# Two groups of weight transfers get later due times in a kernel whose order a list schedule makes

## The chip, the cores and the metric

The kernel runs on one core of a Trainium2 chip. Its time is device microseconds of one execution. A measurement is the median of several executions; three of the kernel before gave 621.62 us (621.21 to 625.1).

## The reference

One decoder layer in float32 on 512 tokens of width 1024: a mixing part (retention heads beside sparse attention) with an output projection, and a gated feed-forward part with a short causal convolution. What the change touches lies in the second half:

```python
mix = jnp.concatenate([y_ret, y_nsa], axis=-1) @ w_out[l]
x = x + rms_norm(mix, norm_mix_post[l])
h = rms_norm(x, norm_ffn_pre[l])
x = x + rms_norm(conv_ffn(h, ffn_w_up[l], ffn_conv[l], ffn_w_down[l]), norm_ffn_post[l])

def conv_ffn(x, w_up, conv_w, w_down):        # w_up: 1024 x 5632, w_down: 2816 x 1024
    u = x @ w_up
    u = depthwise_causal_conv(u, conv_w)       # width 3
    gate, val = jnp.split(u, 2, axis=-1)
    return (jax.nn.gelu(gate) * val) @ w_down
```

## The kernel before

**Arithmetic.** Each float32 matrix is split into a rounded high part (a copy on ScalarE, ACT) and the rest as a low part (a subtraction on VectorE, DVE), and each product is three matmuls: high by high, high by low, low by high.

**Order.** The body doesn't issue instructions. It records operations in a `_Plan`, and `schedule` (L262) orders them: each engine (TensorE as PE, ACT, DVE, GpSimd as POOL, SyncE as SP) has a clock, each operation a cost from `cost`, and of the operations that could start within 20 ns (`SLACK`, L32) of an engine's earliest one the plan takes that with the lowest rank, which within this part of the kernel is the one written first. `emit` then issues each engine's instructions in that order, and the hardware runs each engine's queue strictly in it. So an assumed time shows in the program only as an order: an instruction that the plan believed ready can stand in a queue ahead of one that is ready in fact.

**Due times of transfers.** A transfer's issue costs 475 ns on SP and 1000 ns on POOL. Then it is due at (L368, L369)

```python
dma = max(dma, op.end) + nbytes / (175.0 if "accum_op" in k else 350.0)
op.end = dma + (4000 if e == POOL else 2000) + op.late
```

in nanoseconds, with bytes per nanosecond as the divisors. `op.late` is what `plan.late` was when the operation was recorded (L191); nothing else reads it. `plan.late` is 0 but for the loads of the up stage, where it is 800 (`LATE`, L1386).

**Stage h2.** After the attention part, `wo1(t)` (L1179) makes the second half of the output projection for the 128 tokens of t, 24 matmuls. It squares and sums the result on ACT (`junk<-wo`), and goes on to the norm (`r`, with a power on POOL), the residual sum (`mix<-mix,r,xres`), the square of that (`xres<-mix`), and the next norm (`xres<-mix,r,wpre`). `h2(t)` (L1216) transposes that on PE (`tp<-cn,xres`) into `h2h` and `h2l`. In PE's order of rank wo1 of the later t and the first up products stand behind, and can fill in.

**First up weights.** `ws` (L1342, L1343) loads four blocks of the up weights, 512 KB each, on SP's queue into tile `raw` (two buffers) and splits each: three in one piece (`wh<-raw` on ACT, `wl<-raw` on DVE), the second in two pieces (`w<-raw`, `w<-raw,w`). They are recorded behind wo1 and h2. `up` (L1240) multiplies with them, for column blocks 0 and 1 of gate and value.

**Up stage.** The 20 remaining pairs of column blocks, i = 2 to 21, are made by seven products each (a Strassen form), in the order 1, 2, 6, 5, 7, 3, 4 (`strassen`, L1310), 12 matmuls each. In the trace they are `X<-h2h,b`, `G<-h2h,b`, `X<-T,b`, `G<-T,b`, `X<-T,b`, `G<-h2h,b`, `X<-h2h,b`. The seventh, named "4", uses the tile `w["4"]` (tag av, four buffers, which the tiles a of a11 and a12 share). `loads(i+1)` (L1283) is recorded ahead of the products of i; it issues three transfers on SP and four on POOL, 256 KB each. Two of POOL's add into s1 and s3. The third, here called the casting transfer, copies the second half of the value weights into `w["4"][:, 1]` and rounds it on the way. Behind it ACT writes its negative into `w["4"][:, 0]`, and the fourth, an accumulating transfer, adds the unrounded weights to that, which leaves the low part. `prep` (L1299) makes the parts of the other six products on ACT and DVE (`b<-b`).

**Down stage.** `t_sums`, `product` and what follows do the same for the down weights. The same schedule orders it.

Of the kernel before, what the change touches and what calls it, by code (L numbers as in the profile page):

```python
# [402 lines left out]
def _body(ctx, tc, io, out, soff, coff):  # L403
# [5 lines left out]
    plan = _Plan(nc)  # L409
# [6 lines left out]
    def nm(s):  # L416
        cnt[0] += 1
        return f"{s}_{cnt[0]}"

    def s4(shape, dt=F32, n="s"):  # L420
        return plan.tile(gp, shape, dt, nm(n), "s4", 12)
# [4 lines left out]
    def vv(shape, dt=F32, n="v"):  # L426
        return plan.tile(gp, shape, dt, nm(n), "vv", 2)
# [23 lines left out]
    def acc(n="acc"):  # L451
        return plan.tile(pp, [P, 512], F32, nm(n), "acc", 4)
# [7 lines left out]
    def copy(o, i, scale=None, engs="A"):  # L460
        k = {} if scale is None else {"scale": scale}
        alts = {}
        if "A" in engs:
            alts[ACT] = ("activation", (o, i, AF.Copy), k)
        for c, e in (("D", DVE), ("P", POOL)):
            if c in engs and scale is None:
                alts[e] = ("tensor_copy", (o, i), {})
            elif c in engs and e == POOL:
                alts[e] = ("tensor_tensor", (o, i, scale.to_broadcast(list(o.shape))), {"op": ALU.mult})
            elif c in engs:  # L470
                alts[e] = ("tensor_scalar", (o, i, scale, None), {"op0": ALU.mult})
        plan.add(alts)

    def f(ap):
        return ap.bitcast(F32)
# [34 lines left out]
    def nextw(src, a, b, eng=dve_pool, **k):  # L510
        return splitw(loadw(src, a, b, **k), eng=eng)
# [136 lines left out]
    def transpose4(bank, src):  # L648
        m = bank("tp").rearrange("p (a b) -> p a b", a=4)
        for q in range(4):  # L650
            transpose(m[:, q, :], src(q))
        return m
# [497 lines left out]
    def rawtile(shape=(P, 2, 512)):  # L1150
        return plan.tile(st, list(shape), F32, nm("raw"), "raw", 2)

    def rows(src, a, b):

        return [[x[:, k, :] for k in range(a)] for x in nextw(src, a, b, eng=dve)]

    def rows2(src, a, b, alloc):

        raw, n = rawtile((P, a, b)), a // 2
        sync.dma_start(raw, src)  # L1160
        parts = [], []
        for q in range(2):
            hi, lo = (alloc([P, n, b], F32R, "w") for _ in range(2))
            copy(hi, raw[:, q * n:q * n + n])
            dve.tensor_tensor(lo, raw[:, q * n:q * n + n], f(hi), op=ALU.subtract)
            for k in range(n):
                parts[0].append(hi[:, k, :])
                parts[1].append(lo[:, k, :])
        return parts
# [9 lines left out]
    def wo1(t):  # L1179
        ts = slice(t * P, (t + 1) * P)  # L1180
        a = acc("wo1")
        for j in range(4):
            for b in range(2):
                mm3(a, yh[j][:, b, ts], yl[j][:, b, ts], w1p[j][0][b], w1p[j][1][b],
                    j == 0 and b == 0, j == 3 and b == 1)
        act.activation(junk, a, AF.Square, accum_out=sm2[:, t, 1:2])
        r = tiny([P, 6], "r1")
        dve.tensor_tensor(r[:, 0:1], sm2[:, t, 0:1], sm2[:, t, 1:2], op=ALU.add)
        dve.tensor_scalar(r[:, 0:1], r[:, 0:1], 1.0 / D, 1e-6, op0=ALU.mult, op1=ALU.add)
        rsqrt(r[:, 1:2], r[:, 0:1], 1)  # L1190
        xr = (vv if t < 2 else s4)([P, D], n="xres")
        sync.dma_start(xr, io["x"][ts, :])
        dve.tensor_tensor(mix[t][:, 512:1024], a, wpost[:, 512:1024], op=ALU.mult)
        for c in range(2):
            cs = slice(512 * c, 512 * c + 512)
            dve.scalar_tensor_tensor(mix[t][:, cs], mix[t][:, cs], r[:, 1:2], xr[:, cs], op0=ALU.mult, op1=ALU.add)
            act.activation(xr[:, cs], mix[t][:, cs], AF.Square, accum_out=r[:, 4 + c:5 + c])
        spills.append(sync.dma_start(io["x2"][ts, :], mix[t]))
        dve.tensor_tensor(r[:, 2:3], r[:, 4:5], r[:, 5:6], op=ALU.add)
        dve.tensor_scalar(r[:, 2:3], r[:, 2:3], 1.0 / D, 1e-6, op0=ALU.mult, op1=ALU.add)  # L1200
        rsqrt(r[:, 3:4], r[:, 2:3], 1)
        for c in range(2):
            cs = slice(512 * c, 512 * c + 512)
            dve.scalar_tensor_tensor(xr[:, cs], mix[t][:, cs], r[:, 3:4], wpre[:, cs], op0=ALU.mult, op1=ALU.mult)
        hns[t] = xr
# [10 lines left out]
    def h2(t):  # L1216
        ts = slice(t * P, (t + 1) * P)
        rs = slice(t % 2 * P, t % 2 * P + P)
        if t == 2:
            t13.extend(vv([P, 4, HT], n="T") for _ in range(2))  # L1220
        for q in range(2):
            m = transpose4(mps, lambda k: hns[t][:, (4 * q + k) * P:(4 * q + k + 1) * P])
            copy(h2h[q][:, :, ts], m)
            dve.tensor_tensor(h2l[q][:, :, ts], m, f(h2h[q][:, :, ts]), op=ALU.subtract)
            if t < 2:
                for a in range(2):
                    copy(hb[q][a][:, :, rs], m[:, 2 * a:2 * a + 2, :])
            elif q:
                dve.tensor_tensor(t13[1][:, :, rs], t13[1][:, :, rs], m, op=ALU.subtract)
            else:  # L1230
                for a in range(2):
                    k = slice(2 * a, 2 * a + 2)
                    dve.tensor_tensor(t13[0][:, k, rs], m[:, k, :], hb[0][a][:, :, rs], op=ALU.subtract)
                copy(t13[1][:, :, rs], m)
# [45 lines left out]
    def blk(pool, tag, bufs, dt=F32R):  # L1280
        return plan.tile(pool, [P, 2, 4, P], dt, nm("b"), tag, bufs)

    def loads(i):  # L1283
        g, v = io["wup"][i, 0], io["wup"][i, 1]
        a, s13 = blk(gp, "av", 4, F32), blk(st, "raw", 2, F32)
        w = {"4": blk(gp, "av", 4)}
        a11, a12, s1, s3 = a[:, 0], a[:, 1], s13[:, 0], s13[:, 1]
        sync.dma_start(a11, g[:, 0:4])
        sync.dma_start(s1, v[:, 0:4])
        sync.dma_start(a12, g[:, 4:8])  # L1290
        pool.dma_start(s1, v[:, 4:8], accum_op=ALU.add)
        copy(s3, a11, scale=-1.0)
        pool.dma_start(s3, v[:, 0:4], accum_op=ALU.add)
        pool.dma_start(w["4"][:, 1], v[:, 4:8])
        copy(w["4"][:, 0], f(w["4"][:, 1]), scale=-1.0)
        pool.dma_start(w["4"][:, 0], v[:, 4:8], accum_op=ALU.add)
        return a11, a12, s1, s3, w
# [39 lines left out]
    for t in range(NT):  # L1337
        wo1(t)
        h2(t)
    ws = [rows(io["wup"][0, 0], KT, P), rows2(io["wup"][0, 1], KT, P, pt),  # L1340
          rows(io["wup"][1, 0], KT, P), rows(io["wup"][1, 1], KT, P)]
    ab = [acc("up") for _ in range(4)]  # L1342
    for c0 in (0, 256):  # L1343
        for i in range(4):
# [41 lines left out]
    LATE = 800  # L1386
    plan.late = LATE
    nxt = loads(PL)
    plan.late = 0
    for i in range(PL, NF):  # L1390
        now = prep(*nxt)
        if i == PL:
            glu(1, ab[2], ab[3])
        if i + 1 < NF:
            plan.late = LATE
            nxt = loads(i + 1)
            plan.late = 0
        else:
            uv = u_parts(0), v_parts(0)
        glu(i, *strassen(i, now))  # L1400
# [129 lines left out]
    late = [pair[:, 0], pair[:, 1], s4([P, 2, 512], n="late")]  # L1530
# [46 lines left out]
```

## Time and profile before

| | us |
|---|---|
| median of three runs | 621.62 |
| the profiled execution | 626.48 |
| its span | 624.7 |
| outside the span | 1.8 |
| PE busy | 606.3 |
| DVE busy | 536.8 |
| ACT busy | 426.6 |
| POOL busy | 173.5 |

The profiled execution is 4.86 us above the median. On the page matmuls are pipelined, so the busy time of PE is no measure of its peak; the idle time of PE, by what ended it, is read from the waits. Nearly every instruction is issued from line 398 (`emit`), so groups are told apart by tiles, and where a tile name is shared (`b`), by form and place in time.

### The profile page before, as it was taken

Reading aid. Unit: us, or ns where it says so; the run is one execution under the profiler, and the core shown is the slowest. Engines: PE = TensorE matmul, PEld = TensorE weight load, DVE = VectorE, ACT = ScalarE, POOL = GpSimd, SP = SyncE. Lnnn points to the kernel's source line nnn. Section 1 sums busy time; section 2 is a strip of 40 time slices with the busy share of each in tenths; the row PEclk is TensorE's granted clock in tenths of the full one; section 3 lists DMA queues with packets and bytes.
Section 4 is the critical chain, followed back from the end, with each engine's and each line's share of the span. In section 5 each row is a group of like instructions: output and inputs, shape, how many; then the busy total and the mean of one; then the engine's idle time right before and its main releaser. Section 6 shows DMA issues by size and latency. Waiting matters only on the chain. (4 is left out here: it accounts for less than half of the span.)

```text
span 624.7 us, 10841 instructions
## 1 busy us (share of the span) xinstructions
PE 606.3 (97%) x3782; PEld 537.1 (86%) x3782; DVE 536.8 (86%) x1142; ACT 426.6 (68%) x872; POOL 173.5 (28%) x200
## 2 busy tenths in 40 slices
PE   8998999999999999999999999999999999999995
PEld 5787988888878888789999999999999987787884
DVE  5589877997888885589999989999999999889994
ACT  6735657778998645475867767675777667678761
POOL 0003532533215320032123232324241222231070
PEclk9999899999999999999999999999999999999999
DMA  8762366525126517447467877788868579997722
GB/s 277 298 239 88 135 169 147 124 40 129 35 68 134 137 35 269 164 147 179 93 143 176 180 190 168 182 176 194 204 148 198 121 187 216 238 214 247 268 91 102
DMA packets 42103, 102.31 MB, mean 164 GB/s; under 512 B 4672, under 2 KB 5056, under 8 KB 42048
## 3 DMA queue, kind: packets, MB, share of 16 engines
q0 software_dynamic: 18576, 41.16, 33.8%
q1 hardware_dynamic: 23184, 60.06, 27.9%
q8 instruction: 30, 0.49, 0.3%
q10 hardware_dynamic: 288, 0.39, 0.2%
q14 instruction: 25, 0.20, 0.1%
HBM read 97.40 MB, written 4.19 MB: 163 GB/s over the span
## 5 line engine op out<-in xcount | busy, mean ns | idle before, releaser
L398 DVE TENSOR_TENSOR b<-b,b 128x512 fp32r<-128x512 f32 (+1 forms) x160 | 103.8, 683 | 2.8 <-ACT b L398 1.7
L398 POOL DMA_DIRECT2D b<-wup x80 | 63.5, 930 | 153.3 <-ACT b L398 82.8
L398 ACT ACTIVATE b<-b 128x512 fp32r<-128x512 f32 (+1 forms) x160 | 92.2, 623 | 12.4 <-DMA b<-wup 5.3
L398 PE MATMUL acc<-wl,xh 128*128 128x512 f32 (+1 forms) x192 | 72.8, 384 | 0.6 <-DVE wl L398 0.6
L398 PE MATMUL acc<-wh,xh 128*128 128x512 f32 (+1 forms) x192 | 72.4, 385 | 0.3 <-ACT kc L398 0.3
L398 PE MATMUL acc<-wh,xl 128*128 128x512 f32 (+1 forms) x192 | 72.6, 383 | 0.0
L398 PE MATMUL G<-h2h,b 128*128 128x256 f32 x320 | 64.6, 284 | 0.9 <-ACT b L398 0.9
L398 PE MATMUL X<-T,b 128*128 128x256 f32 x480 | 64.9, 284 | 0.2
L398 PE MATMUL X<-h2h,b 128*128 128x256 f32 x320 | 61.4, 284 | 0.5 <-DVE X L398 0.5
L398 PEld LDWEIGHTS X<-T,b 128*128 128x128 f32 x480 | 60.5, 192 | 0.8 <-DVE b L398 0.6
L398 DVE TENSOR_TENSOR wl<-raw,wh 128x1024 fp32r<-128x1024 f32 (+1 forms) x40 | 48.8, 1221 | 9.9 <-ACT wh L398 9.7
L398 PEld LDWEIGHTS G<-h2h,b 128*128 128x128 f32 x320 | 52.9, 192 | 1.3 <-ACT b L398 1.3
L398 ACT ACTIVATE wh<-raw 128x1024 fp32r<-128x1024 f32 (+2 forms) x43 | 43.1, 1008 | 15.9 <-issue 6.4
L398 PEld LDWEIGHTS X<-h2h,b 128*128 128x128 f32 x320 | 51.4, 192 | 1.0 <-DVE X L398 0.9
L398 PE MATMUL G<-h2l,b 128*128 128x256 f32 x160 | 45.3, 283 | 0.0
L398 PE MATMUL X<-h2l,b 128*128 128x256 f32 x160 | 45.3, 283 | 0.0
L398 PEld LDWEIGHTS acc<-wh,xh 128*128 128x128 f32 x192 | 36.5, 191 | 6.5 <-ACT kc L398 0.7
L398 PEld LDWEIGHTS acc<-wl,xh 128*128 128x128 f32 x192 | 36.6, 191 | 6.4 <-DVE wl L398 1.4
L398 PEld LDWEIGHTS acc<-wh,xl 128*128 128x128 f32 x192 | 36.7, 191 | 5.2
L398 ACT ACTIVATE P<-P,nmx 128x256 f32<-128x256 f32 (+3 forms) x64 | 35.2, 551 | 6.6 <-DVE nmx L398 6.5
L398 PE MATMUL d<-wl,ah 128*128 128x512 f32 x88 | 34.4, 394 | 2.4 <-DVE wl L398 2.4
L398 POOL DMA_DIRECT2D T<-wdn x21 | 18.1, 878 | 57.0 <-ACT T L398 49.8
(298 smaller groups left out, 1646.9 us busy)
## 6 DMA issues: line engine op xcount, KB each, us to landing
b<-wup POOLq DMA_DIRECT2D x80, 256.0 KB, 5.2
b<-wup SPq DMA_DIRECT2D x60, 256.0 KB, 5.1
raw<-wdn SPq DMA_DIRECT2D x15, 512.0 KB, 5.8
T<-wdn POOLq DMA_DIRECT2D x21, 256.0 KB, 6.3
T<-wdn SPq DMA_DIRECT2D x10, 256.0 KB, 5.7
xnat<-x SPq DMA_DIRECT2D x4, 512.0 KB, 7.1
raw<-w_nq SPq DMA_DIRECT2D x4, 512.0 KB, 6.0
raw<-w1k SPq DMA_DIRECT2D x4, 512.0 KB, 5.2
```

The source lines that it names most:

```text
L398: i = getattr(getattr(self.nc, op.eng), method)(*a, **k)
```

## The change

The casting transfer of `loads` is recorded with a `late` of 4500 ns where it had 800, and the four loads of the first up weights with 2000 where they had 0. No operation is added or taken away, none changes its size, queue, buffers or recorded place. The plan's due times change, and with them the order that it makes from there on.

```diff
@@ loads(i)
         copy(s3, a11, scale=-1.0)
         pool.dma_start(s3, v[:, 0:4], accum_op=ALU.add)
+        late, plan.late = plan.late, max(plan.late, 4500)
         pool.dma_start(w["4"][:, 1], v[:, 4:8])
+        plan.late = late
         copy(w["4"][:, 0], f(w["4"][:, 1]), scale=-1.0)
         pool.dma_start(w["4"][:, 0], v[:, 4:8], accum_op=ALU.add)
@@ _body
     for t in range(NT):
         wo1(t)
         h2(t)
+    plan.late = 2000
     ws = [rows(io["wup"][0, 0], KT, P), rows2(io["wup"][0, 1], KT, P, pt),
           rows(io["wup"][1, 0], KT, P), rows(io["wup"][1, 1], KT, P)]
+    plan.late = 0
     ab = [acc("up") for _ in range(4)]
```

## Rows read from the trace of the kernel before

**Rows 1.** The page's first part: busy us of an engine, its share of the span, and its instructions.

```profile
PE 606.3 (97%) x3782; PEld 537.1 (86%) x3782; DVE 536.8 (86%) x1142; ACT 426.6 (68%) x872; POOL 173.5 (28%) x200
```

**Rows 2.** Busy time by stretches (us from the span's start): length, then busy us of PE, PEld, DVE, ACT, POOL with instructions, granted clock, DMA share, GB/s. The stretches are stage h2, the rest of it with the first up products, the up stage in part, and the down stage.

```profile
262.00:277.00 15.00, 13.50 (x68) 10.80 (x67) 11.86 (x24) 10.38 (x25) 3.77 (x6) 1.00 0.41 152
277.00:302.00 25.00, 24.82 (x207) 24.57 (x206) 23.08 (x42) 17.17 (x34) 7.77 (x10) 1.00 0.65 157
...
402.00:452.00 50.00, 49.48 (x409) 49.03 (x409) 47.67 (x82) 35.68 (x70) 15.89 (x20) 1.00 0.80 181
...
525.00:614.00 89.00, 86.63 (x379) 70.37 (x378) 81.35 (x131) 62.73 (x112) 25.41 (x17) 1.00 0.73 206
```

**Rows 3.** What PE waited for from 245 us to the end (the waits of 245 to 302, of 300 to 510, and of 502 to 625 us): us in total, times, longest.

```profile
PE tp L398 <- DVE xres L398: 1.5, 1, 1.5
...
PE G L398 <- ACT b L398: 0.9, 2, 0.6
PE X L398 <- DVE X L398: 0.5, 1, 0.5
...
PE d L398 <- DVE wl L398: 2.4, 3, 1.0
PE d L398 <- ACT wh L398: 0.8, 2, 0.7
```

**Rows 4.** The first and the second of the four loads of the first up weights: the issue in the timeline of SP (start, duration), and in the view of the DMA issues its KB and us from issue to landing. The third and the fourth took 3.2 and 3.1.

```profile
251.41 0.33 SPq L398 DMA_DIRECT2D raw<-wup  x1
raw<-wup SPq DMA_DIRECT2D x1, 512.0 KB, 3.3
253.22 0.33 SPq L398 DMA_DIRECT2D raw<-wup  x1
raw<-wup SPq DMA_DIRECT2D x1, 512.0 KB, 5.7
```

**Rows 5.** Timeline of ACT in stage h2: start, duration, what, and idle time before with what ended it.

```profile
254.83 1.06 ACT L398 ACTIVATE wh<-raw 128x1024 fp32r<-128x1024 f32 x1 [0.25 <-DMA raw<-wup]
258.98 0.63 ACT L398 ACTIVATE w<-raw 128x512 fp32r<-128x512 f32 x1 [3.09 <-DMA raw<-wup]
259.52 0.58 ACT L398 ACTIVATE junk<-wo 128x512 bf16<-128x512 f32 x1
```

**Rows 6.** Timeline of PE there: the first and the last of the 24 matmuls of `wo1(0)`, the last one ahead of the transposes, the first transposes, and the first up product.

```profile
252.01 0.39 PE L398 MATMUL wo<-wh,yh 128*128 128x512 f32 x1
...
257.22 0.39 PE L398 MATMUL wo<-w,yl 128*128 128x512 f32 x1
...
264.25 0.39 PE L398 MATMUL wo<-wh,yh 128*128 128x512 f32 x1
266.14 0.66 PE L398 MATMUL tp<-cn,xres 128*128 128x128 f32 x4 [1.50 <-DVE xres L398]
...
277.44 0.28 PE L398 MATMUL up<-h2h,wh 128*128 128x256 f32 x1
```

**Rows 7.** Timeline of DVE there: the chain from the sum of squares to the transposes' input, with the two subtractions of the second load.

```profile
259.64 0.69 DVE L398 TENSOR_TENSOR w<-raw,w 128x512 fp32r<-128x512 f32 x1 [2.50 <-ACT w L398]
260.25 0.15 DVE L398 TENSOR_TENSOR r<-sm 128x1 f32<-128x1 f32 x1
260.32 0.68 DVE L398 TENSOR_TENSOR mix<-wo,wpost 128x512 f32<-128x512 f32 x1
260.92 0.14 DVE L398 TENSOR_SCALAR r<-r 128x1 f32<-128x1 f32 x1
260.98 0.68 DVE L398 TENSOR_TENSOR w<-raw,w 128x512 fp32r<-128x512 f32 x1
262.11 1.42 DVE L398 SCALAR_TENSOR_TENSOR mix<-mix,r,xres 128x512 f32<-128x512 f32 x2 [0.44 <-POOL r L398]
```

**Rows 8.** Transfers of the up stage: the median of the 80 on POOL's queue (issue to landing), then the casting transfer that ACT waited for, its issue in POOL's timeline and its time to landing, and ACT's row behind it.

```profile
b<-wup POOLq DMA_DIRECT2D x80, 256.0 KB, 5.2
...
415.41 1.52 POOL L398 DMA_DIRECT2D b<-wup  x1
b<-wup POOLq DMA_DIRECT2D x1, 256.0 KB, 9.9
...
425.32 1.15 ACT L398 ACTIVATE b<-b 128x512 fp32r<-128x512 f32 x2 [0.93 <-DMA b<-wup]
```

**Rows 9.** What ACT waited for on transfers in the up stage (300 to 510 us), all kinds of them together: us in total, times, longest.

```profile
ACT b L398 <- DMA b<-wup: 4.9, 5, 1.5
```

**Rows 10.** Three of the accumulating transfers into `w["4"]`: issue in POOL's timeline, us to landing, and the PE row that holds the first matmul of product 4 that reads the low part.

```profile
353.64 0.85 POOL L398 DMA_DIRECT2D b<-wup  x1
b<-wup POOLq DMA_DIRECT2D x1, 256.0 KB, 7.0
363.14 0.40 PE L398 MATMUL X<-h2h,b 128*128 128x256 f32 x2
...
427.06 1.21 POOL L398 DMA_DIRECT2D b<-wup  x1
b<-wup POOLq DMA_DIRECT2D x1, 256.0 KB, 7.7
435.83 0.40 PE L398 MATMUL X<-h2h,b 128*128 128x256 f32 x2
...
477.58 0.85 POOL L398 DMA_DIRECT2D b<-wup  x1 [0.15 <-issue]
b<-wup POOLq DMA_DIRECT2D x1, 256.0 KB, 7.5
486.58 0.40 PE L398 MATMUL X<-h2h,b 128*128 128x256 f32 x2
```

## The prediction

> **What bounds the kernel now.** I read the page's first part, then the stretches, then the waits of PE, then the rows around each wait that the change can reach. PE is busy 97% of the span [rows 1], at the full clock from stage h2 on [rows 2], and DVE is close behind it in the up stage, 47.67 of 50 us [rows 2]. So PE's queue sets the time, and an edit that adds no work can gain only what PE idles. From 245 us to the end that is 1.5 us in stage h2, 0.9 + 0.5 in the up stage and 2.4 + 0.8 in the down stage [rows 3]: 6.1 us. What the plan places ahead of the first of the four loads (251.41, [rows 4]) keeps its order. One per cent of 621.62 is 6.2 us, about what a measurement of this kernel can tell from no change, so a gain of that size would need every one of these waits gone. A loss has no such bound, since an order can be made worse anywhere behind the first changed due time.
>
> **The first up weights.** By the plan's rule a 512 KB load on SP is due 0.475 + 524288/350 = 1.5 + 2.0, together 3.97 us, behind the start of its issue; with the change, 5.97. The trace has 3.3 for the first load and 5.7 for the second [rows 4]. So the old due time is right for all but the second, and the new one covers that too.
>
> What the 1.7 us between due and landed cost can be followed. The second load is issued at 253.22 [rows 4], due by the old rule at 257.19, landed in fact at 258.9. The 24 matmuls of `wo1(0)` run from 252.01 to 257.22 + 0.39 = 257.61 [rows 6], so the plan believed the split's copy ready 0.4 us ahead of the sum of squares, and put it first in ACT's queue. ACT waits 3.09 us for the load, copies at 258.98, and squares at 259.52 [rows 5], 1.9 us after PE was done. Behind the squares come the norm and the residual sum on DVE, at 262.11 [rows 7], and at the chain's end the transposes, for which PE idles 1.50 us [rows 6].
>
> With 2.0 us more the load is due at 259.19, and the squares stand ahead of its copy. The first load's copy may stay ahead of them (due 251.41 + 5.97 = 257.38), but that one ends at 254.83 + 1.06 = 255.9 in fact [rows 5], so it holds up nothing. The squares then start at about 257.7 and not at 259.52. DVE's links to the residual sum take 262.11 − 260.25 = 1.9 us [rows 7], which puts it at 260.3. Where the two subtractions of the second load (0.69 and 0.68 us, [rows 7]) slip in between, they start at 258.96 + 0.63 = 259.6 and end at 260.9. So the sum comes 1.2 to 1.8 us sooner, the transposes are ready at 264.3 to 264.9, and the last matmul ahead of them starts at 264.25 [rows 6] and is followed by the next after 0.23 us (257.22 − 252.01 over 23 steps, [rows 6]). PE's wait falls from 1.50 to between 0 and 0.4. The plan itself believes in a later chain and may put more matmuls of the next wo1 ahead of the transposes, which covers the rest. I take 1.4 us. The bounds are 0, where the load lands in 3.3 us and there was no wait to lose, and 1.9, all that the squares come sooner.
>
> What moves behind is the split itself, some 1 to 2 us later in ACT's and DVE's order. Its users, the first up products, begin at 277.44, 11 us behind the transposes [rows 6], so this is free as long as wo1 and h2 fill PE until then; without that cover it costs those 2 us. The third and fourth load wait for raw buffers that the first and second give back, so SP may issue them up to 2 us later; both are hidden by the same 11 us. From 277 us PE is busy 24.82 of 25 us [rows 2].
>
> **The casting transfers.** By the rule 256 KB on POOL are due 1.0 + 0.75 + 4.0 + 0.8 = 6.55 us behind the start of the issue; with 4.5 in place of 0.8, 10.25. So 20 times one copy on ACT and one accumulating transfer on POOL stand 3.7 us later in their queues. In the trace POOL's transfers of the stage land in 5.2 us in the median, but the slowest casting one that I read took 9.9, and ACT stood 0.93 us in front of its copy [rows 8]. The new due time covers that one. All waits of ACT on transfers in this stage are 4.9 us [rows 9], and those of PE on anything 1.4 [rows 3]. So the gain lies between 0 and 1.4. I take 0.4, near the lower end, since the rows show one casting transfer late by 0.93 and tie no wait of PE to it directly.
>
> The Trainium skill speaks against this edit: by "DMA: Bandwidth & Descriptors", section "Anatomy of one DMA — SWDGE (gpsimd) path", a transfer on POOL's path takes about 2.0 us plus its bytes over 436 GB/s, some 2.6 us for 256 KB (an estimate by that page). The trace doesn't agree, with 5.2 in the median and 9.9 at worst [rows 8]. By the page the old due time would be too late already, the gain of this edit 0, and the sum 0.4 us smaller.
>
> The price is the accumulating transfer's. It was issued at 353.64, 427.06 and 477.58 and landed at 360.6, 434.8 and 485.1; PE read the low part at 363.14, 435.83 and 486.58 [rows 10]. That leaves 2.5, 1.0 and 1.5 us, all less than 3.7. With PE's order as it is, PE would wait 1.2 + 2.7 + 2.2 = 6.1 us. But the plan moves product 4 as well when it believes its weights late, and takes products 1 and 2 of the next pair in between, 12 matmuls each, whose weights `prep` has made by then. And an accumulating transfer is due after 1.0 + 1.5 + 4.0 + 0.8 = 7.3 us by a rule that is left alone, against 7.0, 7.7 and 7.5 measured [rows 10], so the new order is right within 0.4 us. I take 0, with 6.1 as the other end.
>
> POOL's queue goes on in order. Behind each accumulating transfer wait the s1 and s3 sums of the next pair. If it stands later, they can stand ahead of it, which helps `prep`; if it doesn't move and ACT's copy does, they wait up to 3.7 us behind it. POOL is busy 28% [rows 1], so only order and not load matters there.
>
> **The down stage** gets no new due time but another start, and its 3.2 us of PE waits [rows 3] can go or come again. I take 0 and bounds of 3.2 us either way.
>
> **Sum.** 1.4 + 0.4 = 1.8 us off the profiled execution's 626.48, of which 624.7 is span. The median lies 4.86 us below that execution; I take the same 1.8 us off it: 621.62 − 1.8 = 619.8 us.
>
> **Rivals.**
> - *Nothing to gain.* The second load's 5.7 us was that execution's, since the three others land in 3.1 to 3.3, and the casting transfers land early enough, as the page's rule would have it. For it: 5.2 against 6.55 us of due time, and 4.86 us between this execution and the median. Against it: ACT's 3.09 and 0.93 us in front of transfers. Time: 621.62 with both terms 0.
> - *The down stage falls worse.* For it: its order is remade from another start, and DVE's `wl` is what PE waits for there, with DVE 81.35 of 89 us busy [rows 2]. Against it: nothing in it is touched. Time: 619.8 + 3.2 = 623.0.
> - *The seventh product's low part comes late, and the kernel is slower.* Place: product 4 in the up stage, in the iterations where the margin is under 3.7 us. Price: 6.1 us for the three, less the 1.4 of stage h2: 626.3. It decides once PE's order keeps product 4 where it is while the copy on ACT moves, and goes beyond 627.8 if more iterations than these three run short. For it: margins of 1.0 to 2.5. Against it: the plan knows of the wait and moves the product.
>
> **How the numbers follow.** Forecast (0.5 to 5 us faster, likeliest 1.8): 0.60. Nothing to gain: 0.15. Down stage worse: 0.12. Late low part: 0.13, half of it beyond 1%. The range runs from 616.2 (1.9 + 1.4 and two thirds of the down stage's 3.2, that is 5.4, off 621.62) to 626.3, the late low part's price; about 0.05 lies below and 0.08 above. Faster by over 1% (under 615.4) would need all 6.1 us of waits: 0.03. Slower by over 1% (above 627.8): 0.07. Within: 0.90.
>
> **What would show it.** In the changed profile: `junk<-wo` ahead of the first `w<-raw` on ACT, at about 1 us behind the last matmul of `wo1(0)` or less; the wait of `tp` on `xres` gone or under 0.4; ACT's 0.93 in front of a casting copy gone. Against me: PE waits of X on b or on a transfer in the up stage, the accumulating transfer landing within 0.5 us of product 4, or a down stage with much more than 3.2 us of waits on `wl` and `wh`.

## The result, and the profile after

| | before | after |
|---|---|---|
| median of 20 runs, us | 623.63 (619.80 to 625.66) | 619.88 (617.21 to 621.70) |
| ratio of the runs | | 0.9949, 95% interval 0.9931 to 0.9966 |
| the profiled execution, us | 626.48 | 620.87 |
| its span, us | 624.7 | 619.1 |

The change makes the kernel 0.5% faster, 3.2 us (2.1 to 4.3). The forecast was 1.8 us and 619.8 us. The gain is nearly twice the forecast. That the absolute time was met within 0.1 us is luck: the 20 runs of before have a median 2 us above that of the three runs from which the forecast was taken.

**Stage h2.** ACT's timeline after (start, us of one, engine, line, operation, tiles, count, and in brackets the wait ahead of it and on what), against [rows 5]:

```profile
253.59 1.06 ACT L398 ACTIVATE wh<-raw 128x1024 fp32r<-128x1024 f32 x1
256.64 0.60 ACT L398 ACTIVATE junk<-wo 128x512 bf16<-128x512 f32 x1 [1.99 <-PE wo L398]
...
257.70 1.16 ACT L398 ACTIVATE w<-raw 128x512 fp32r<-128x512 f32 x2 [0.37 <-DMA raw<-wup]
```

The squares stand ahead of the copy of the second load, and what ended ACT's wait is now PE. That load still took 5.5 us, as the view of the transfers after shows (tile from input, queue, count, KB each, us from issue to landing):

```profile
raw<-wup SPq DMA_DIRECT2D x1, 512.0 KB, 5.5
```

DVE's timeline after, against [rows 7], shows where the gain in the chain is partly given back: both subtractions of the second load slip in ahead of the residual sum.

```profile
257.36 0.16 DVE L398 TENSOR_TENSOR r<-sm 128x1 f32<-128x1 f32 x1 [1.45 <-ACT junk L398]
257.44 0.68 DVE L398 TENSOR_TENSOR mix<-wo,wpost 128x512 f32<-128x512 f32 x1
258.04 0.15 DVE L398 TENSOR_SCALAR r<-r 128x1 f32<-128x1 f32 x1
258.37 1.29 DVE L398 TENSOR_TENSOR w<-raw,w 128x512 fp32r<-128x512 f32 x2 [0.18 <-ACT w L398]
259.58 1.41 DVE L398 SCALAR_TENSOR_TENSOR mix<-mix,r,xres 128x512 f32<-128x512 f32 x2
```

PE's timeline after, against [rows 6]: the first matmul of wo1, the last ahead of the transposes, the transposes, and the first up product.

```profile
250.94 0.39 PE L398 MATMUL wo<-wh,yh 128*128 128x512 f32 x1
...
265.90 0.39 PE L398 MATMUL wo<-w,yh 128*128 128x512 f32 x1
266.13 0.60 PE L398 MATMUL tp<-cn,xres 128*128 128x128 f32 x4
...
274.56 0.28 PE L398 MATMUL up<-h2h,wh 128*128 128x256 f32 x1
```

The transposes start no sooner than before, but PE doesn't wait for them: 67 matmuls of wo1 stand ahead of them and not 55, one every 0.23 us. From the first wo1 matmul to the first up product it is 274.56 − 250.94 = 23.62 us, against 277.44 − 252.01 = 25.43. (The 1.07 us by which the first matmul is sooner lies ahead of anything that the change touches: up to there every engine has the same order in both kernels.)

**What PE waits for** after, in the stretches of [rows 3] (us in all, times, the longest). In the first of them (245 to 302 us) nothing is left; this is the second, 300 to 510 us:

```profile
PE G L398 <- ACT b L398: 0.3, 1, 0.3
PE X L398 <- DVE b L398: 0.3, 1, 0.3
PE G L398 <- DVE b L398: 0.2, 1, 0.2
```

and the third, the down stage from 502 us:

```profile
PE d L398 <- ACT wh L398: 1.3, 3, 0.8
PE d L398 <- DVE wl L398: 1.1, 2, 0.8
```

Together 3.2 us, against 6.1.

**The up stage.** Busy time by stretches, before and then after (columns as in [rows 2]; the third stretch of before is shown there):

```profile
302.00:352.00 50.00, 49.53 (x409) 48.92 (x408) 49.32 (x86) 36.30 (x71) 11.95 (x16) 1.00 0.68 161
352.00:402.00 50.00, 49.41 (x408) 48.80 (x407) 45.94 (x79) 34.20 (x67) 15.71 (x20) 1.00 0.79 181
...
452.00:502.00 50.00, 50.00 (x419) 50.00 (x418) 48.45 (x85) 35.45 (x69) 13.53 (x17) 1.00 0.72 161
```

```profile
302.00:352.00 50.00, 49.09 (x401) 48.20 (x401) 49.63 (x86) 36.10 (x71) 16.29 (x21) 1.00 0.73 157
352.00:402.00 50.00, 50.00 (x419) 50.00 (x418) 48.38 (x83) 36.27 (x71) 16.11 (x21) 1.00 0.84 187
402.00:452.00 50.00, 50.00 (x419) 50.00 (x419) 47.48 (x83) 36.48 (x70) 15.29 (x20) 1.00 0.86 186
452.00:502.00 50.00, 50.00 (x418) 49.96 (x417) 47.46 (x81) 35.30 (x66) 11.86 (x15) 1.00 0.74 164
```

The count of matmuls says more here than the busy time. A stretch of 50 us holds up to 419 of them. Before, three of the four fell short by 10 or 11; after, only the first does, by 18. In 200 us that is 1657 matmuls against 1645, 12 more, at 0.12 us each (50/419) 1.4 us, and with it 1.4 us sooner at 502. ACT's waits on transfers in this stage (300 to 510 us) fell; the row of after, against [rows 9]:

```profile
ACT b L398 <- DMA b<-wup: 2.2, 3, 1.5
```

All three of these are the plain copies of a11 into s3, not casting copies, as their form in ACT's timeline after shows (f32 from f32, the casting copies write fp32r):

```profile
327.80 0.64 ACT L398 ACTIVATE b<-b 128x512 f32<-128x512 f32 x1 [1.54 <-DMA b<-wup]
...
369.79 0.63 ACT L398 ACTIVATE b<-b 128x512 f32<-128x512 f32 x1 [0.28 <-DMA b<-wup]
...
389.63 0.63 ACT L398 ACTIVATE b<-b 128x512 f32<-128x512 f32 x1 [0.42 <-DMA b<-wup]
```

The accumulating transfer that had the least margin in [rows 10], after: its issue in POOL's timeline,

```profile
420.61 1.19 POOL L398 DMA_DIRECT2D b<-wup  x1
```

its row in the view of the transfers,

```profile
b<-wup POOLq DMA_DIRECT2D x1, 256.0 KB, 7.0
```

and the first matmul that reads it, in PE's timeline:

```profile
431.34 0.40 PE L398 MATMUL X<-h2h,b 128*128 128x256 f32 x2
```

It lands at 427.6, 3.7 us ahead of the matmul that reads it; before it was 1.0. PE has product 4 in its old place there. What grew is the lead of the issue over the reader, from 8.8 to 10.7 us. The smallest margin of the 20 pairs is now that of the seventh, shown by the issue, the time to landing, and PE's row, whose second matmul (372.30) is the reader:

```profile
364.28 0.86 POOL L398 DMA_DIRECT2D b<-wup  x1 [1.93 <-ACT u L398]
b<-wup POOLq DMA_DIRECT2D x1, 256.0 KB, 7.2
...
372.18 0.52 PE L398 MATMUL X<-h2h,b 128*128 128x256 f32 x3
```

That leaves 0.8 us.

### The profile page after: what moved, and what is told of

The parts are those of the page before. It is cut to its first block, busy times and chain, and to the rows that moved or that the text cites. A ratio compares the mean times of both kernels' runs of the same rounds, so it can differ in the third digit from the quotient of the medians.

```text
span 619.1 us, 10856 instructions
## 1 busy us (share of the span) xinstructions
PE 604.2 (98%) x3782; PEld 536.8 (87%) x3782; DVE 538.3 (87%) x1141; ACT 428.4 (69%) x872; POOL 163.5 (26%) x201
## 5 line engine op out<-in xcount | busy, mean ns | idle before, releaser
L398 DVE TENSOR_TENSOR wl<-raw,wh 128x1024 fp32r<-128x1024 f32 (+1 forms) x40 | 50.5, 1266 | 9.9 <-ACT wh L398 9.7
L398 DVE SCALAR_TENSOR_TENSOR v<-G,sm,v 128x511 f32<-128x511 f32 (+1 forms) x40 | 29.8, 744 | 5.5 <-ACT v L398 5.5
```

What stands on the lines that cost most here:

```text
L398: i = getattr(getattr(self.nc, op.eng), method)(*a, **k)
```

## The experiments

Theory: the change is two separate edits of order. Each takes an ACT copy that waits for a transfer out of the way of something that PE needs, and the gains add up. Rivals: all of it comes from one edit; the due time has to cover the real landing; what counts is the order on POOL's queue; a later low part of product 4 costs part of the gain. Diffs are against the changed kernel where nothing else is said, and each ratio is to executions of the kernel before that were made along with it.

### One edit at a time

Only the first up weights late:

```diff
-        late, plan.late = plan.late, max(plan.late, 4500)
+        late, plan.late = plan.late, max(plan.late, 0)
```

> Only the first up weights get the later due time (2000); the casting transfers keep 800. Theory (two separate gains that add up): the squares of wo1(0) stand ahead of the second load's copy on ACT, PE's wait for xres in stage h2 (1.5 us before) is under 0.2, the time from the first wo1 matmul to the first up product is about 23.6 us (25.43 before, 23.62 with the whole change), and the kernel is 1.5 to 2.0 us faster than before, a ratio of 0.997 (0.9960 to 0.9985). The up stage keeps its two irregular places, PE waits of about 1.4. Rival (the second load's late landing belonged to one execution, and all of the gain is the casting transfers'): ratio 1.000, within 0.001.

Measured: ratio 0.9991 (0.9968 to 1.0014). In its profile stage h2 runs from 250.91 to 274.53, 23.62 us, without a wait of PE, and the up stage still has 0.9 us of waits on ACT's b. So the mechanism did what was said. The time gained is 0.6 us by the ratio, at most 2.0, and by the ratio alone it may be nothing.

Only the casting transfers late:

```diff
-    plan.late = 2000
+    plan.late = 0
     ws = [rows(io["wup"][0, 0], KT, P), rows2(io["wup"][0, 1], KT, P, pt),
```

> Only the casting transfers get the later due time (4500); the first up weights keep 0. Theory: the 1.5 us wait in stage h2 is there again, the first G product to the last product of the up stage takes about 203 us (205.1 before, 203.0 with the whole change), and the kernel is 1.5 to 2.5 us faster than before, a ratio of 0.997 (0.9955 to 0.9985). Rival of the first run: the whole gain, 0.995. Rival two (the later accumulating transfer makes product 4 wait, and only stage h2 gained): ratio 1.000 or above, with PE waits of X in the up stage.

Measured: ratio 0.9970 (0.9946 to 0.9994), 1.9 us. The wait in stage h2 was there again, with less than half its size, as this kernel's timeline of PE shows:

```profile
262.73 0.39 PE L398 MATMUL wo<-wh,yh 128*128 128x512 f32 x1
263.79 0.66 PE L398 MATMUL tp<-cn,xres 128*128 128x128 f32 x4 [0.67 <-DVE xres L398]
```

The order on ACT was that of before, with the copy ahead of the squares, but the second load landed after 4.8 us and not 5.7. The stage took from 250.49 to 275.09, 24.60 us. So the first edit is worth 1.0 us in that execution and 1.8 in the profile of before: its size hangs on when that one load lands. The profiles of all fourteen kernels of this document bear that out. The three without the edit have the same order on every engine in this stage, and it took 25.43, 24.60 and 24.36 us with landings of 5.7, 4.8 and 4.7. The eleven with it had landings from 4.5 to 5.6, and the stage took 23.61 to 23.69 in every one. So the edit is worth 0.7 to 1.8 us of stage time, and takes the landing's spread out of it. The product of both ratios is 0.9961, inside the interval of the whole change, so that the two gains add up is consistent with the times and not shown by them alone.

A smaller due time for the first up weights, with the casting transfers at 800: `plan.late = 1000`.

> The first up weights with 1000 in place of 2000, the casting transfers with 800. The plan then still puts the squares of wo1(0) ahead of the second load's copy, but the first load's copy is believed 1 us sooner. Theory (the order of squares and copy on ACT is the whole gain of this edit): the same as with 2000 alone, 1.5 to 2.0 us faster than before, ratio 0.997. Rival (the due time has to cover the real landing of 5.7 us, and 3.97 + 1.0 = 4.97 doesn't): half of it or less, ratio 0.9985 to 1.000.

Measured: ratio 0.9997 (0.9975 to 1.0020), which neither separates it from 0.9991 nor from no gain. The profile does: stage h2 took 23.69 us without a wait, the same as with 2000, though 4.97 us of due time covers neither the landing of 5.7 before nor the 5.1 of this execution. What counts is that the squares stand ahead of the copy; the due time need not be true.

### The price of a late low part

```diff
         copy(w["4"][:, 0], f(w["4"][:, 1]), scale=-1.0)
+        late, plan.late = plan.late, -2900
         pool.dma_start(w["4"][:, 0], v[:, 4:8], accum_op=ALU.add)
+        plan.late = late
```

> The whole change, but the accumulating transfer behind the casting one gets -2900 in place of 800, so that the plan believes its landing as early as before: the copy on ACT and the issue on POOL stand 3.7 us later, while product 4 isn't moved. It prices the case of the prediction's slower rival. By the margins of before (1.0 to 2.5 us in the tightest three) product 4 waits up to 6 us in all, the up stage takes up to 209 us, and the ratio to before lies between 0.998 and 1.008. If the order of PE matters less than that, because the margins in the new order are wider, the ratio is that of the whole change, 0.995.

Measured: ratio 0.9986 (0.9965 to 1.0007). PE's waits in its up stage, 300 to 510 us (us in all, times, the longest):

```profile
PE X L398 <- DMA b<-wup: 1.8, 2, 1.3
PE X L398 <- ACT u L398: 1.4, 1, 1.4
PE G L398 <- ACT b L398: 0.3, 1, 0.3
```

The first line is the mechanism of the prediction's slower rival: product 4's third matmul waits for its weights, in the same kernel's timeline of PE (the longer of the two waits, in the seventh pair):

```profile
371.15 0.28 PE L398 MATMUL X<-h2l,b 128*128 128x256 f32 x1
372.75 0.50 PE L398 MATMUL X<-h2h,b 128*128 128x256 f32 x2 [1.32 <-DMA b<-wup]
```

It costs 1.8 us in two places, not 6.1 in three. The second line has another cause, an ACT copy of down weights that waited 1.24 us ahead of u at 501 us. Against the whole change this kernel loses about 0.0037, or 2.3 us. In PE's order the changed kernel differs from this one in the fifth, sixth and seventh pair (and by one matmul at 330 us): there the plan, when it is told, lets the first matmuls of the next pair go ahead of product 4's third. The two waits here, at 351.0 and 372.8 us, are in the fifth and the seventh. So that is where product 4 has to move along with its transfer; in the other pairs it needn't.

### Other due times for the casting transfers

4500 was tried against 2000, 3000, 6000 and 8000, each in the whole change. The theories at that point: the order on POOL, where from the seventh pair on with 4500 each accumulating transfer stands behind both sums and the casting transfer of the next pair; or a due time that covers the landing.

> The whole change with 2000 in place of 4500 for the casting transfers, so they are due 7.75 us behind the start of their issue. In the order that this gives, each accumulating transfer of a pair stands on POOL's queue ahead of the s3 sum, the s1 sum or the casting transfer of the next pair, in no fixed pattern; with 4500 it stands behind all three, in every pair from the eighth on. Theory one (what helps is that pattern: sums and casting transfer of the next pair are issued before the queue waits for ACT's copy): little of the up stage's gain, 202 us or more from the first G product to the first down product (202.64 before, 200.79 with 4500), ratio 0.998 to 1.000. Theory two (the due time has to cover the landing; most land in under 7.75): most of the gain, 201.3 us or less, ratio 0.995 to 0.997.

> The whole change with 3000 in place of 4500: due 8.75 us behind the start of the issue. The pattern on POOL is still broken in most pairs. Theory one: 202 us or more for the stretch, ratio 0.998 to 1.000. Theory two: only a transfer of 9 us or more is missed, so 201 us or less, ratio 0.995 to 0.996.

> The whole change with 6000 in place of 4500: due 11.75 us behind the start of the issue. The pattern on POOL is the regular one from the third pair on. Both theories: as with 4500, about 200.8 us for the stretch, ratio 0.994 to 0.997. The rival with the late low part would have the accumulating transfer 1.5 us later still, PE waits of X on transfers, and 1 to 3 us lost against 4500.

> The whole change with 8000 in place of 4500: due 13.75 us behind the start of the issue, 3.5 us more than with 4500. The pattern on POOL is regular. Theory one: as with 4500, about 201 us for the stretch, ratio 0.994 to 0.997, since the plan moves product 4 along. The rival with the late low part: PE waits for product 4's weights in many pairs, the stretch takes 203 us or more, ratio 0.999 or above.

| late | ratio (95% interval) | ACT's waits on transfers, 300 to 510 us: total, times, longest |
|---|---|---|
| 2000 | 1.0076 (1.0035 to 1.0117) | 16.4, 11, 2.9 |
| 3000 | 0.9965 (0.9940 to 0.9990) | 3.5, 6, 1.3 |
| 4500 | 0.9949 (0.9931 to 0.9966) | 2.2, 3, 1.5 |
| 6000 | 1.0003 (0.9975 to 1.0031) | 5.2, 5, 2.9 |
| 8000 | 0.9939 (0.9921 to 0.9958) | 1.0, 2, 0.8 |

(2000 has 7 executions, which lie far apart, 622.69 to 631.00 us; the others have 12 or more.)

Both theories fall. POOL's order is broken with 3000 and the time is good; it is regular with 6000 and the time is no better than before. And the time doesn't fall with the due time. What goes along with the time in all five is how long ACT stands in front of a transfer. That total is no measure by itself: with the first up weights alone at 1000 it is 2.7 us and the ratio 0.9997. It matters what stands behind the wait. With 2000, PE's waits of the stage show the link,

```profile
PE G L398 <- ACT p L398: 4.1, 7, 1.4
PE G L398 <- DVE b L398: 1.8, 2, 1.6
```

and ACT's timeline of the same kernel shows the place of the longest wait for a transfer:

```profile
434.50 0.63 ACT L398 ACTIVATE b<-b 128x512 f32<-128x512 f32 x1 [2.92 <-DMA b<-wup]
435.04 0.37 ACT L398 ACTIVATE p<-G 128x256 f32<-128x256 f32 x1
```

and PE's timeline what it held up, the first matmul of product 3:

```profile
435.46 0.39 PE L398 MATMUL G<-h2h,b 128*128 128x256 f32 x1 [1.42 <-ACT p L398]
```

The transfer is not a casting one but SP's load of a11, whose due time (0.475 + 0.75 + 2.0 + 0.8 = 4.0 us) the change leaves alone. SP's 60 loads of these weights land after 5.1 us in the median before and 5.9 after. Its copy into s3 stands in front of the copy of p out of PSUM, and PE can't begin product 3 until p is copied.

With 6000 one such place makes the difference. ACT's longest wait is again for a11, with the copy u behind it that PE needs (ACT's timeline, then PE's):

```profile
389.71 0.63 ACT L398 ACTIVATE b<-b 128x512 f32<-128x512 f32 x1 [2.94 <-DMA b<-wup]
390.25 0.37 ACT L398 ACTIVATE u<-X 128x256 f32<-128x256 f32 x1
...
390.67 2.03 PE L398 MATMUL X<-T,b 128*128 128x256 f32 x12 [1.74 <-ACT u L398]
```

And the wait cost more than its own length. Behind it the granted clock fell from 1.00 to 0.50, the lower of its two levels (1.2 GHz and not 2.4), as the stretch of 392 to 394 us shows (columns as in [rows 2]):

```profile
392.00:394.00 2.00, 2.00 (x12) 2.00 (x11) 1.02 (x2) 1.59 (x3) 0.07 (x1) 0.50 0.91 143
```

There 16 matmuls followed each other after 0.21 us and not 0.12, some 1.5 us more. From its first product to its last the up stage took 219.3 us in this profile and 216.0 in that of 4500. The 3.3 us between them are about what this one place cost: 1.9 us of pause from one matmul to the next (388.65 to 390.67, less 0.12) and the 1.5.

So the rival that the prediction lacked is this one: a new due time for one transfer shifts another ACT copy, whose transfer the plan still believes early, into the place where it hurts.

### That link by itself

In the kernel with 2000 only the order on ACT was changed, behind the plan, in the eight places where the s3 copy stands right ahead of p or u:

```diff
     def emit(self, tc):
-            for op in self.schedule():
+            for op in self.copies_first(self.schedule()):
...
+    def copies_first(self, order):   # moves an s3 copy behind the copy of p or u that follows it on ACT
```

> The kernel with 2000 for the casting transfers, with one thing changed behind the plan: in the eight places where ACT's copy of a11 into s3 stands right ahead of the copy p or u out of PSUM, the two change places. No due time and nothing on PE, DVE, POOL or SP moves. Theory three (ACT's copies of a11 wait for SP's loads, 16.5 us in all with 2000, and hold up the copy of p behind them, for which product 3 waits on PE): PE's wait of G on p goes from 4.1 us to under 0.5, and the kernel gets 4 to 6 us faster than that one's 1.0076, a ratio of 0.998 to 1.002. Rival (the accumulating transfers that stand ahead of the sums of the next pair are what costs): the waits turn up at DVE or at product 6 and 7, ratio 1.005 or above.

Measured: ratio 1.0038 (1.0013 to 1.0063), 0.0038 or 2.4 us below the kernel without the exchange, but the two intervals overlap, so that the time fell isn't clear of noise. Of PE's waits in the up stage these are the longest that are left:

```profile
PE G L417 <- DVE b L417: 1.1, 2, 0.9
PE X L417 <- DVE X L417: 0.5, 1, 0.5
PE X L417 <- DMA b<-wup: 0.4, 1, 0.4
```

The wait of G on p, 4.1 us, is gone altogether, ACT's waits on transfers are down from 16.4 to 6.0, and from its first product to its last the up stage takes 219.6 us in this profile against 224.2. So the link from the copy of a11 to PE's wait is shown by the profiles; what it is worth in time is not. The expected ratio was 0.998 to 1.002 and was missed. The stage is still 3.6 us longer than with 4500, and where that comes from stays open.

The same exchange in the kernel with 8000, 13 places:

> The same exchange in the kernel with 8000 for the casting transfers, where it applies in 13 places. ACT waited there only 1.0 us for a11 in two places, and PE 0.2 for u. Theory three: nothing or up to 0.5 us gained, ratio 0.993 to 0.995. A ratio above 0.997 would say that a later s3 copy has a price of its own.

Measured: ratio 0.9956 (0.9931 to 0.9981), not to be told from 0.9939. Where ACT hardly waits for a11, the exchange does nothing that can be measured. With 8000 the transfers themselves came sooner, which the order on ACT doesn't explain: SP's 60 loads landed after 3.4 us in the median, against 5.9 with 4500. Why isn't shown.

### The other transfer made late

The kernel before, with a11 late and nothing else:

```diff
+        late, plan.late = plan.late, 3000
         sync.dma_start(a11, g[:, 0:4])
+        plan.late = late
```

> The kernel before with one due time changed: SP's load of a11 gets 3000 in place of 800, so it is due 6.2 us behind the start of its issue and not 4.0. The first up weights keep 0 and the casting transfers 800. Theory three: ACT's waits on a11 (4.0 us in four places before) go under 1 us; the casting copy's 0.9 may stay. PE's waits in the up stage were 1.4 us, so 0.5 to 1.5 us are gained, ratio 0.9975 to 0.9995. Rival (the casting transfers alone made the up stage faster): ratio 1.000 or above.

Measured: ratio 0.9965 (0.9939 to 0.9991), and ACT's waits on transfers in the up stage 1.9 us in three places (4.9 before). That is as much as the casting transfers alone give. With the first up weights at 2000 as well:

> The first up weights with 2000 as in the change, SP's load of a11 with 3000, and the casting transfers left at 800: the change with another transfer of the up stage made late in place of the casting one. If the gains of the two stages add up, and if in the up stage it matters only that ACT stops waiting for transfers: ratio 0.994 to 0.997, stage h2 at 23.6 us, PE's wait for xres gone, ACT's waits on transfers in the up stage under 2.5 us. If the casting transfers' due time is what the whole change needs: 0.997 or above.

Measured: ratio 0.9948 (0.9925 to 0.9971), ACT's waits 1.6 us in four places. It can't be told from the change, nor can the kernel with 8000 (0.9939): neither is shown to be better. The casting transfers' due time is one way among several to an order in which ACT doesn't wait.

## Why the prediction was right, point by point

- **What bounds the kernel.** Right: PE's waits from 245 us on fell from 6.1 to 3.2, the profiled span by 5.6 us, of which 1.07 lies ahead of the change. Faster by over 1% stayed out of reach. A difference of 1% was said to be about what a measurement can tell; with 20 executions of each the interval was 0.2% either way.
- **The first up weights, 1.4 us.** The mechanism held step by step: squares first, the two subtractions in between, more matmuls of wo1 as cover, the wait gone. The size is that of the executions: 1.8 us of stage time against the profile of before, 1.0 against the kernel with only the other edit, and 0.6 (−0.9 to 2.0) in the ratio of 0.9991. The term took one execution's landing of 5.7 us for all of them; the fourteen profiles have 4.5 to 5.7. That also answers the rival by which the late landing belonged to one execution: the second load was the slowest of the four in every profile, and the others took 3.1 to 3.5.
- **The casting transfers, 0.4 us.** This term was mis-sized: the edit alone gave 1.9 us (0.4 to 3.4). This is the larger part of why the gain was nearly twice the forecast. The step "near the lower end, since the rows show one casting transfer late by 0.93 and tie no wait of PE to it directly" looked for the gain at the casting copies. Their wait did go, but the new order also let ACT wait less for a11 (4.0 of the 4.9 us before were four copies of a11, 0.93 the one casting copy), and a later a11 alone gave as much. How the 1.9 us divide between the two isn't shown. And the bound of 1.4 us from PE's waits was too low: a matmul is drawn 0.28 us long and the next starts after 0.12, so a pause of up to 0.16 us doesn't show as a wait, and a longer one shows 0.16 short. The count of matmuls from 302 to 502 us shows 1.4 us gained, where the waits fell by 0.6 (1.4 to 0.8).
- **The page's rule.** By the Trainium skill, "DMA: Bandwidth & Descriptors", section "Anatomy of one DMA — SWDGE (gpsimd) path", the edit should have been worth nothing. The transfers on POOL land in 5.0 us in the median after the change, about twice the 2.6 estimated from that page, and the interval of the edit by itself (0.9946 to 0.9994) leaves a gain of nothing out. The gain is no test of the page's landing time, though, since part of it came through SP's loads.
- **The late low part, 6.1 us or nothing.** Nothing came of it, as forecast, but only in part for the reason given. The plan moved product 4 in three of the 20 pairs, the fifth to the seventh, and with it kept in place there the wait appeared, at 1.8 us; that the whole 2.3 us of lost time is its own isn't shown. In the two tightest places of before, the 13th and the 18th pair, product 4 stayed, and the margin grew since the transfer is issued earlier ahead of its reader. The price was also added up over too few places: the trace of before has two more margins under 3.7 us, 2.3 and 2.6, and with them the same sum gives 8.6 and not 6.1.
- **The down stage, 0.** Waits of 2.4 us after, 3.2 before; nothing more can be said of it.

## What to carry to other kernels

In a queue that runs in order, a due time is worth what it puts behind what, not how true it is: look for the instruction that waits for a transfer with something behind it that the bounding engine needs, and move that. A new due time for one transfer reorders all that follows, and two neighbouring values can differ by 1% with opposite sign; so read which waits an order makes, and what stands behind them, before holding a value to be right, and try several. Where matmuls are pipelined, count them in equal stretches rather than add up the waits.

## What the runs showed of the hardware

The same stretch of program, in the same order, takes different times: the first wo1 matmul, ahead of which every engine has the same order in all fourteen kernels, starts at 248.96 in one profile and at 252.10 in another. The row of PE's timeline in the kernel with 2000 and the exchange on ACT:

```profile
248.96 0.39 PE L417 MATMUL wo<-wh,yh 128*128 128x512 f32 x1
```

and in the kernel with 6000:

```profile
252.10 0.39 PE L398 MATMUL wo<-wh,yh 128*128 128x512 f32 x1
```

So single profiles of this kernel differ by 3 us for no reason in the program, as much as the whole change is worth, and stages have to be compared by their own lengths.
